# Column-quarter matmuls of a decoder step's sample group, issued in fours

## The chip, the cores and the metric

The kernel runs on one core of a Trainium2 chip. The metric is the device time of one execution in microseconds (us), from the core's first instruction to its last and what lies around them; lower is better. TensorE (PE) multiplies and transposes, VectorE (DVE), ScalarE (ACT) and GpSimd (POOL) work on elements, SyncE (SP) issues most of the DMAs.

## The reference

One step of a decoder layer for two groups that share the weights: a prompt group (1 x 1024 tokens, positions 0 to 1023) and a sample group (8 samples x 4 tokens, each with a past of 512 positions in pages of 128, and 256 memory tokens of its own). All inputs are float32.

```python
def layer_forward(x, p, layer, h0_re, h0_im, conv_prev, mem_k, mem_v, attend):
    xn = rms_norm(x, p['ln1_g'])
    proj = xn @ p['w_in']
    ...
    ssm_out, h_re, h_im = s5_mixer(u, h0_re, h0_im, p)
    ...
    o = attend(q, k, v, lam)
    o = rms_norm(o, p['subln_g']) * (1.0 - lam0)
    mixed = jnp.concatenate([ssm_out, o.reshape(bsz, t, ATTN_WIDTH)], axis=-1)
    x = x + mixed @ p['w_out']
    xn = rms_norm(x, p['ln2_g'])
    cq = rms_norm((xn @ p['ca_wq']).reshape(bsz, t, CA_HEADS, CA_HEAD_DIM), p['ca_q_norm_g'])
    s = jnp.einsum('bqhd,bmhd->bhqm', cq, mem_k.astype(cq.dtype)).astype(f32) * (CA_HEAD_DIM ** -0.5)
    pr = jax.nn.softmax(s, axis=-1).astype(x.dtype)
    co = jnp.einsum('bhqm,bmhd->bqhd', pr, mem_v.astype(x.dtype)).reshape(bsz, t, D_MODEL)
    x = x + co @ p['ca_wo']
    ...
    x = x + (jax.nn.silu(conv) * (xn @ p['ffn_wv'])) @ p['ffn_wd']
    return x, k, v, h_re, h_im, buf[:, t:]
```

`attend` is differential attention with 4 heads of two maps: softmax of each map, the first less `lam` times the second, times the values. For the sample group, keys and values are the 4 pages that the page table names, and the 4 new tokens.

## The kernel before, in words

The program is written as generators ("streams"). Each yields a cost after a piece of work, and a driver takes next a piece of the stream that is furthest behind its rate; a scheduler then puts the instructions of each engine in an order of their own, and each engine works through its order strictly. A stream's place in the driver decides roughly where its instructions come to lie, its tiles' buffers decide when its loads can start.

The prompt group's large matmuls run as three passes of a shortened float32 format, 128 x 128 weights over 256 to 512 columns (`mm3`, lines 180 to 182). The sample group's attention is done in full float32, and its stationary operand has 32 columns for each sample (4 heads x 2 maps x 4 tokens, or 4 heads x 4 tokens padded): the matmul of sample b uses one quarter of TensorE's columns, `tile_position=(0, 32 * (b % 4))`, and writes 32 partitions of the result. A float32 matmul is recorded as two passes. Four places do this:

- `keys` (line 1369), in `sample_attention`: for each of two groups `s` of four samples and for each sample, two pages at a time. A page is gathered by SP (`pg`, five buffers `PGB`), TensorE transposes it into `pt`, ScalarE copies that to `KT`, and after every second page four matmuls (one a head) of 256 columns accumulate the scores `Sp`.
- `values` (line 1422), for each sample, four pages (also `pg`) and the new tokens `vs_`: five matmuls of 512 columns accumulate `Op`, each issued as its page comes. `values(0)` runs beside `keys(1)`; `soft` lies between keys and values of a group.
- `sample_keys` (line 1784), cross-attention, for each of four heads and each sample: the memory keys `kt` (three buffers) are loaded by SP, transposed, copied to `KT` by ScalarE; two matmuls of 256 columns accumulate `Ssm`.
- `sample_values` (line 1857), cross-attention's output: 32 loads of `vt`, 128 x 512 each, issued by GpSimd, six ahead; each has one matmul of 512 columns into `Op` (line 1870).

Beside the first two run the prompt's last attention heads, the memory's keys and values (`memory_kv`, `pjm`, whose weights `mraw` come by SP) and the state-space scan (`yp`, `wp`, `kp`); beside the third the prompt's cross-attention (`pp`, `S`, `po`); beside the fourth the output projection (`wo_stage`, `pp`), whose last third waits for `sample_values`. The matmuls of `kp` (line 965, `ssm_setup`) use column quarters too: they go through the four quarters with two matmuls on each.

Of the kernel before, what the change touches and what calls it, by code (L numbers as in the profile page):

```python
# [21 lines left out]
NS = 32  # L22
# [16 lines left out]
TB = [(0, 384), (384, 384), (768, 288)]  # L39
TILES = [(128 * t, 128) for t in range(8)] + [(1024, 32)]  # L40


class Boosted:
    """An engine whose instructions the scheduler ranks boost[0] places earlier."""
# [23 lines left out]
def hymba_step(ctx: ExitStack, tc: tile.TileContext, A: dict, O: dict, upto=99, dbg=None):  # L68
# [7 lines left out]
    def par(*streams):  # L76
        # each stream: a generator of costs, its rate, the share it starts behind, its boost
# [109 lines left out]
    class Carve:  # L187
        """Small tiles cut from a few large ones; a tag names one region."""
# [132 lines left out]
    def ssm_params(st, ps):  # L321
# [58 lines left out]
        # cos and sin of the chunk angle times 0..15, and times 0, 16, ..., 112  # L380
# [725 lines left out]
    # sample group: the recurrence step by step  # L1106
# [77 lines left out]
    # keys and values of the prompt's memory  # L1184
# [78 lines left out]
    # differential attention of the sample group over its pages  # L1263
    sc = {}

    def sample_tables(sa):
# [29 lines left out]
        # columns: the past, new keys for the first four samples, new keys for the last four  # L1296
# [46 lines left out]
    def sample_attention(sa):  # L1343
# [6 lines left out]
        def gather(src, j):  # L1350
            g = sa.tile([128, 512], F32, tag="pg", name="pg", bufs=PGB)
# [17 lines left out]
        def keys(s):  # L1369
            Sp = ps_j.tile([128, PAST], F32, tag="pjb", name="Sp")  # L1370
            Sps.append(Sp)
            for b4 in range(4):
                b = 4 * s + b4
                rows = slice(32 * b4, 32 * b4 + 32)
                for pg in range(NPG):
                    if pg % 2 == 0:
                        KT = sa.tile([128, NH, 256], F32, tag="KT", name="KT", bufs=2)
                    kp_ = gather(kpg, NPG * b + pg)
# [3 lines left out]
                    c = 128 * (pg % 2)  # L1382
                    nc.scalar.copy(KT[:, :, c:c + 128], pt.rearrange("p (h k) -> p h k", h=4))
                    yield 440
                    if pg % 2:
# [219 lines left out]
    if upto <= 4:  # L1605
        return

# [1 line left out]
    pcs = ctx.enter_context(ExitStack())  # L1609
    cqs = pool(pcs, "cqs", 1)  # L1610
    hm = cqs.tile([128, 4], F32, name="hm")
# [499 lines left out]
```

## Time and profile before

| | before |
|---|---|
| device time, median of 3 runs | 1912.89 us (1910.13 to 1913.94) |
| span of the profiled execution, which the page gives as its time | 1912.4 us |
| TensorE busy (weight loads) | 1842.9 us (1649.2 us) |
| VectorE, ScalarE, GpSimd busy | 1144.4, 623.8, 473.8 us |
| moved by DMA | 147.15 MB, mean 77 GB/s |
| mean granted TensorE clock | 0.966 of full speed |

A pass counts as busy until its modelled end, and passes overlap, so a busy share says that TensorE had work and not how much it could have done. The runs of before lie within 0.2% of each other.

### The profile page before, as it was taken

The numbers are of one execution on the slowest core, as the hardware profiler recorded it, in microseconds if no ns is written. First come the engines' busy times: TensorE is split into PE (matmuls) and PEld (weight loads), VectorE is DVE, ScalarE is ACT, GpSimd is POOL, SyncE is SP. The second block draws the span as 40 slices with busy tenths as digits, with TensorE's granted clock in tenths as the row PEclk, the third lists the DMA queues.
The fourth block names the chain that finished last, engine by engine and source line by source line (L and its number), as shares of the span: only waits on it lengthen the run. The fifth ranks groups of instructions, "written<-read, shape, count | busy, mean of one in ns | idle before, by whom it ended". The sixth has DMA issues, their size and how long they took to land. (4 is left out here: it accounts for less than half of the span.)

```text
span 1912.4 us, 29088 instructions
## 1 busy us (share of the span) xinstructions
PE 1842.9 (96%) x11105; PEld 1649.2 (86%) x11105; DVE 1144.4 (60%) x2867; ACT 623.8 (33%) x1425; POOL 473.8 (25%) x547
## 2 busy tenths in 40 slices
PE   7899999889899999999989999999999999999998
PEld 6787897767556799888855999999999999999998
DVE  6976448795876554655452665555656646556554
ACT  6654345545243543344441312112102102112112
POOL 4412321360530024100012333223123123223200
PEclk8888998979799999999999999999999999999999
DMA  7202112134355342322243111011111102102102
GB/s 224 68 28 62 44 48 65 48 108 129 113 147 158 117 145 82 95 85 92 78 154 127 56 37 56 27 52 57 45 34 57 55 23 68 45 23 68 45 23 92
DMA packets 160773, 147.15 MB, mean 77 GB/s; under 512 B 14167, under 2 KB 142067, under 8 KB 160634
## 3 DMA queue, kind: packets, MB, share of 16 engines
q1 hardware_dynamic: 135698, 111.03, 19.2%
q0 software_dynamic: 7232, 18.71, 3.2%
q10 hardware_dynamic: 17704, 15.56, 2.4%
q8 instruction: 87, 1.43, 0.3%
q14 instruction: 52, 0.43, 0.1%
HBM read 120.07 MB, written 25.19 MB: 76 GB/s over the span
## 5 line engine op out<-in xcount | busy, mean ns | idle before, releaser
L54 DVE TENSOR_TENSOR xacc<-xacc,pd 128x384 f32<-128x384 f32 (+1 forms) x264 | 134.9, 518 | 168.7 <-PE pd L182 168.7
L54 ACT CAST whi<-raw 128x1024 fp32r<-128x1024 f32 x74 | 77.5, 1049 | 427.9 <-PE pg L181 332.8
L182 PE MATMUL pv<-Xh,wlo 128*128 128x384 f32 (+1 forms) x528 | 171.3, 325 | 0.3 <-DVE wlo L54 0.3
L180 PE MATMUL pv<-Xh,whi 128*128 128x384 f32 (+1 forms) x528 | 171.6, 325 | 0.0
L180 PE MATMUL pd<-ah,dhi 128*128 128x384 f32 (+1 forms) x528 | 171.2, 325 | 0.1
L180 PE MATMUL pg<-Xh,whi 128*128 128x384 f32 (+1 forms) x528 | 171.2, 324 | 0.0
L181 PE MATMUL pv<-Xl,whi 128*128 128x384 f32 (+1 forms) x528 | 171.1, 324 | 0.0
L182 PE MATMUL pd<-ah,dlo 128*128 128x384 f32 (+1 forms) x528 | 170.9, 324 | 0.0
L181 PE MATMUL pd<-al,dhi 128*128 128x384 f32 (+1 forms) x528 | 170.1, 322 | 0.5 <-DVE al L54 0.5
L181 PE MATMUL pg<-Xl,whi 128*128 128x384 f32 (+1 forms) x528 | 170.6, 323 | 0.0
L182 PE MATMUL pg<-Xh,wlo 128*128 128x384 f32 (+1 forms) x528 | 170.2, 322 | 0.0
L54 DVE TENSOR_TENSOR wlo<-raw,whi 128x1024 fp32r<-128x1024 f32 x74 | 107.0, 1448 | 21.1 <-ACT whi L54 20.8
L180 PE MATMUL pp<-Mh,whi 128*128 128x384 f32 (+1 forms) x336 | 109.2, 328 | 0.9 <-ACT Mh L54 0.9
L181 PE MATMUL pp<-Ml,whi 128*128 128x384 f32 (+1 forms) x336 | 108.5, 326 | 0.8 <-DVE Ml L54 0.8
L182 PE MATMUL pp<-Mh,wlo 128*128 128x384 f32 (+1 forms) x336 | 109.2, 327 | 0.0
L798 POOL TENSOR_TENSOR raw<-raw,GT 128x1024 f32<-128x1024 f32 x30 | 67.0, 2233 | 165.2 <-DMA raw<-in_ffn_wg_dram 99.2
L180 PE MATMUL pj<-whi,Xh 128*128 128x384 f32 (+1 forms) x288 | 105.3, 367 | 1.5 <-DVE mx L54 1.5
L181 PE MATMUL pj<-wlo,Xh 128*128 128x384 f32 (+1 forms) x288 | 103.2, 359 | 0.2
L182 PE MATMUL pj<-whi,Xl 128*128 128x384 f32 (+1 forms) x288 | 103.2, 359 | 0.0
L182 PEld LDWEIGHTS pv<-Xh,wlo 128*128 128x128 f32 x528 | 99.7, 189 | 0.5 <-DVE wlo L54 0.4
L181 PEld LDWEIGHTS pd<-al,dhi 128*128 128x128 f32 x528 | 99.2, 188 | 0.8 <-DVE al L54 0.8
L180 PEld LDWEIGHTS pd<-ah,dhi 128*128 128x128 f32 x528 | 99.0, 188 | 0.9 <-ACT ah L54 0.5
(813 smaller groups left out, 4873.8 us busy)
## 6 DMA issues: line engine op xcount, KB each, us to landing
raw<-in_ffn_wg_dram SPq DMA_DIRECT2D x22, 512.0 KB, 3.8
raw<-in_ffn_wv_dram SPq DMA_DIRECT2D x22, 512.0 KB, 3.8
raw<-in_ffn_wd_dram SPq DMA_DIRECT2D x22, 512.0 KB, 3.6
pg<-in_cache_k_dram SPq DMA_DIRECT2D x32, 256.0 KB, 2.7
pg<-in_cache_v_dram SPq DMA_DIRECT2D x32, 256.0 KB, 3.3
kt<-in_cache_mem_k_dram SPq DMA_DIRECT2D x32, 256.0 KB, 2.8
vt<-in_cache_mem_v_dram POOLq DMA_DIRECT2D x32, 256.0 KB, 3.9
raw<-in_w_in_dram SPq DMA_DIRECT2D x48, 128.0 KB, 2.5
```

The lines of the kernel that those rows point to most:

```text
L54: return f(*a, **k)
L180: nc.tensor.matmul(out, lhsT=wh, rhs=xh, start=start, stop=False)
L181: nc.tensor.matmul(out, lhsT=wh, rhs=xl, start=False, stop=False)
L182: nc.tensor.matmul(out, lhsT=wl, rhs=xh, start=False, stop=stop)
L798: nc.gpsimd.tensor_tensor(out=raw, in0=raw, in1=g.unsqueeze(2).to_broadcast([128, KD, 128]), op=ALU.mult)
```

## The change

Each of the four places now collects the operands of four samples and then issues their matmuls in fours, one on each column quarter, in the order 3, 2, 1, 0 (`QUADS`), under a raised scheduling priority.

- `keys`: the loop over pages is outside, that over the four samples inside. `KT` holds one page of four samples (8 KB a partition); 16 matmuls of 128 columns follow each quad of pages. `pg` has two buffers and not five; `KT`, `V` and `Pm` share one tag, `big`, with two buffers (`KTB`).
- `values`: `V` holds one page of four samples, gathered by four loads; then four matmuls of 512 columns, one a sample.
- `sample_keys`: `KT` holds the keys of four samples in one buffer (`CKB`, which the tile names), `kt` has two buffers and not three, then eight matmuls of 256 columns. `co` has two buffers and not three.
- `sample_values`: 16 loads of 512 KB with four samples x 256 columns (runs of 1 KB in memory and not 2 KB), three buffers, then four matmuls of 256 columns.

The number of transposes, copies and bytes is the same. The diff, cut to these (what is left out are comments):

```diff
@@ -37,11 +37,12 @@
+QUADS = (3, 2, 1, 0)
@@ -1347,8 +1348,9 @@
         npg = A['cache_k'].shape[1]
         pages = {}
 
-        def gather(src, j):
-            g = sa.tile([128, 512], F32, tag="pg", name="pg", bufs=PGB)
+        def gather(src, j, g=None):
+            if g is None:
+                g = sa.tile([128, 512], F32, tag="pg", name="pg", bufs=PGB)
             if j not in pages:
                 pages[j] = nc.sync.value_load(ptab[0:1, j:j + 1], min_val=0, max_val=npg - 1)
             nc.sync.dma_start(out=g, in_=src[bass.ds(pages[j], 1)].rearrange("n s f -> (n s) f"))
@@ -1369,29 +1371,26 @@
         def keys(s):
             Sp = ps_j.tile([128, PAST], F32, tag="pjb", name="Sp")
             Sps.append(Sp)
-            for b4 in range(4):
-                b = 4 * s + b4
-                rows = slice(32 * b4, 32 * b4 + 32)
-                for pg in range(NPG):
-                    if pg % 2 == 0:
-                        KT = sa.tile([128, NH, 256], F32, tag="KT", name="KT", bufs=2)
-                    kp_ = gather(kpg, NPG * b + pg)
+            for pg in range(NPG):
+                KT = sa.tile([128, 4, NH, 128], F32, tag="big", name="KT", bufs=KTB)
+                for b4 in range(4):
+                    kp_ = gather(kpg, NPG * (4 * s + b4) + pg)
                     pt = tp("pt", "td")
                     for h in range(NH):
                         nc.tensor.transpose(pt[:, 128 * h:128 * h + 128], kp_[:, 128 * h:128 * h + 128], ident)
-                    c = 128 * (pg % 2)
-                    nc.scalar.copy(KT[:, :, c:c + 128], pt.rearrange("p (h k) -> p h k", h=4))
+                    nc.scalar.copy(KT[:, b4], pt.rearrange("p (h k) -> p h k", h=4))
                     yield 440
-                    if pg % 2:
-                        for h in range(NH):
-                            nc.tensor.matmul(Sp[rows, 256 * (pg // 2):256 * (pg // 2) + 256], lhsT=Qb[:, h, b, :],
-                                             rhs=KT[:, h, :], start=h == 0, stop=h == NH - 1,
-                                             tile_position=(0, 32 * b4))
-                        yield 500
+                with tc.high_priority():
+                    for h in range(NH):
+                        for b4 in QUADS:
+                            nc.tensor.matmul(Sp[32 * b4:32 * b4 + 32, 128 * pg:128 * pg + 128],
+                                             lhsT=Qb[:, h, 4 * s + b4, :], rhs=KT[:, b4, h, :],
+                                             start=h == 0, stop=h == NH - 1, tile_position=(0, 32 * b4))
+                yield 1000
 
         def soft(s):
             Sp = Sps[s]
-            Pm = sa.tile([128, PAST + NS], F32, tag="Pm", name="Pm")
+            Pm = sa.tile([128, PAST + NS], F32, tag="big", name="Pm", bufs=KTB)
             mx = sa.tile([128, 1], F32, tag="mxs", name="mxs")
             sm_ = sa.tile([128, 1], F32, tag="sms", name="sms")
             mx2 = sa.tile([128, 2], F32, tag="mx2", name="mx2")
@@ -1423,16 +1422,19 @@
             aT = aTs[s]
             yield from until(lambda: 'left' in done)
             Op = ps_x.tile([128, 512], F32, tag="x", name="Op")
-            for b4 in range(4):
-                b = 4 * s + b4
-                for pg in range(NPG + 1):
-                    if pg < NPG:
-                        lh, rh = aT[:, pg, 32 * b4:32 * b4 + 32], gather(vpg, NPG * b + pg)
-                    else:
-                        lh, rh = aT[:NS, NPG, 32 * b4:32 * b4 + 32], vs_
-                    nc.tensor.matmul(Op[32 * b4:32 * b4 + 32, :], lhsT=lh, rhs=rh, start=pg == 0, stop=pg == NPG,
-                                     tile_position=(0, 32 * b4))
-                    yield 240
+            for pg in range(NPG + 1):
+                if pg < NPG:
+                    V = sa.tile([128, 4, 512], F32, tag="big", name="V", bufs=KTB)
+                    rh = [gather(vpg, NPG * (4 * s + b4) + pg, V[:, b4]) for b4 in range(4)]
+                else:
+                    rh = [vs_] * 4
+                yield 10
+                with tc.high_priority():
+                    for b4 in QUADS:
+                        lh = aT[:128 if pg < NPG else NS, pg, 32 * b4:32 * b4 + 32]
+                        nc.tensor.matmul(Op[32 * b4:32 * b4 + 32, :], lhsT=lh, rhs=rh[b4], start=pg == 0,
+                                         stop=pg == NPG, tile_position=(0, 32 * b4))
+                yield 950
             os_ = gp.tile([128, 128], F32, tag="os_", name="os_")
             nc.vector.tensor_scalar(out=os_, in0=Op[:, 0:128], scalar1=hmask[:, 0:1], scalar2=None, op0=ALU.mult)
             for h in range(1, NH):
@@ -1473,7 +1475,7 @@
-    PGB = 5
+    PGB, KTB = 2, 2
@@ -1625,6 +1627,7 @@
+        CKB = 1
@@ -1775,7 +1778,7 @@
                         split(co_h[z][:, t0:t0 + nq], co_l[z][:, t0:t0 + nq], po[:, :nq])
                         yield 6 * nq / 2.4
                         continue
-                    co = ca.tile([128, 384], F32, tag="co", name="co", bufs=3)
+                    co = ca.tile([128, 384], F32, tag="co", name="co", bufs=2)
                     nc.scalar.copy(co[:, :nq], po[:, :nq])
                     d = 256 * h + 128 * z
                     nc.scalar.dma_start(out=coT[d:d + 128, t0:t0 + nq], in_=co[:, :nq])
@@ -1784,22 +1787,25 @@
         def sample_keys(h):
             while h not in queries:
                 yield None
-            for b in range(NB):
-                kt = ca.tile([128, 2, 256], F32, tag="kt", name="kt", bufs=3)
-                nc.sync.dma_start(out=kt, in_=A['cache_mem_k'][0, b, :, h, :].rearrange("(c p) d -> p c d", p=128))
-                pt = ps_t.tile([128, 2, 2, 128], F32, tag="tp", name="pt")
-                for c in range(2):
+            for s in range(2):
+                KT = ca.tile([128, 4, 2, NMEM], F32, tag="KT", name="KT", bufs=CKB)
+                for b4 in range(4):
+                    kt = ca.tile([128, 2, 256], F32, tag="kt", name="kt", bufs=2)
+                    nc.sync.dma_start(out=kt, in_=A['cache_mem_k'][0, 4 * s + b4, :, h, :].rearrange(
+                        "(c p) d -> p c d", p=128))
+                    pt = ps_t.tile([128, 2, 2, 128], F32, tag="tp", name="pt")
+                    for c in range(2):
+                        for z in range(2):
+                            nc.tensor.transpose(pt[:, z, c, :], kt[:, c, 128 * z:128 * z + 128], ident)
+                    nc.scalar.copy(KT[:, b4].rearrange("p z m -> p (z m)"), pt.rearrange("p z c m -> p (z c m)"))
+                    yield 440
+                with tc.high_priority():
                     for z in range(2):
-                        nc.tensor.transpose(pt[:, z, c, :], kt[:, c, 128 * z:128 * z + 128], ident)
-                KT = ca.tile([128, 2, NMEM], F32, tag="KT", name="KT")
-                nc.scalar.copy(KT.rearrange("p z m -> p (z m)"), pt.rearrange("p z c m -> p (z c m)"))
-                yield 440
-                r = 32 * (b % 4)
-                for z in range(2):
-                    nc.tensor.matmul(Ssm[r:r + 32, :], lhsT=Qc[:, z, b, :], rhs=KT[:, z, :],
-                                     start=h == 0 and b < 4 and z == 0, stop=h == NH - 1 and b >= 4 and z == 1,
-                                     tile_position=(0, r))
-                yield 240
+                        for b4 in QUADS:
+                            nc.tensor.matmul(Ssm[32 * b4:32 * b4 + 32, :], lhsT=Qc[:, z, 4 * s + b4, :],
+                                             rhs=KT[:, b4, z, :], start=h == 0 and s == 0 and z == 0,
+                                             stop=h == NH - 1 and s == 1 and z == 1, tile_position=(0, 32 * b4))
+                yield 960
 
         def field_masks():
             pio = ca.tile([128, 1], I32, name="pio", bufs=1)
@@ -1856,24 +1862,26 @@
 
         def sample_values():
             Op = ps_o.tile([128, 1024], F32, name="Op")
-            work = [(s, c, g, b4) for s in range(2) for c in range(2) for g in range(2) for b4 in range(4)]
-
-            def load(s, c, g, b4):
-                vt = wx.tile([128, 512], F32, tag="vt", name="vt", bufs=7)
-                nc.gpsimd.dma_start(out=vt, in_=A['cache_mem_v'][0, 4 * s + b4, 128 * c:128 * c + 128].rearrange(
-                    "m h d -> m (h d)")[:, 512 * g:512 * g + 512])
+            work = [(g, s, c) for g in range(NH) for s in range(2) for c in range(2)]
+
+            def load(g, s, c):
+                vt = wx.tile([128, 4, 256], F32, tag="vt", name="vt", bufs=3)
+                nc.gpsimd.dma_start(out=vt, in_=A['cache_mem_v'][0, 4 * s:4 * s + 4, 128 * c:128 * c + 128].rearrange(
+                    "b m h d -> m b (h d)")[:, :, 256 * g:256 * g + 256])
                 return vt
 
-            vts = [load(*w) for w in work[:6]]
+            vts = [load(*w) for w in work[:3]]
             yield WD
-            for i, (s, c, g, b4) in enumerate(work):
-                nc.tensor.matmul(Op[32 * b4:32 * b4 + 32, 512 * g:512 * g + 512],
-                                 lhsT=PT[:, c, s, 32 * b4:32 * b4 + 32], rhs=vts[i],
-                                 start=s == 0 and c == 0, stop=s == 1 and c == 1, tile_position=(0, 32 * b4))
-                if i + 6 < len(work):
-                    vts.append(load(*work[i + 6]))
-                yield 250
-            os_ = wx.tile([128, 256], F32, tag="vt", name="os_", bufs=7)
+            for i, (g, s, c) in enumerate(work):
+                with tc.high_priority():
+                    for b4 in QUADS:
+                        nc.tensor.matmul(Op[32 * b4:32 * b4 + 32, 256 * g:256 * g + 256],
+                                         lhsT=PT[:, c, s, 32 * b4:32 * b4 + 32], rhs=vts[i][:, b4],
+                                         start=s == 0 and c == 0, stop=s == 1 and c == 1, tile_position=(0, 32 * b4))
+                if i + 3 < len(work):
+                    vts.append(load(*work[i + 3]))
+                yield 500
+            os_ = wx.tile([128, 256], F32, tag="os", name="os_", bufs=1)
             nc.vector.tensor_scalar(out=os_, in0=Op[:, 0:256], scalar1=hm[:, 0:1], scalar2=None, op0=ALU.mult)
             for h in range(1, NH):
                 nc.vector.scalar_tensor_tensor(out=os_, in0=Op[:, 256 * h:256 * h + 256], scalar=hm[:, h:h + 1],
```

How it moves instructions on TensorE is seen in its order, at two places. The first is in the second half of the attention values (`values(1)`); line 1433 is the matmul `Op` of before, `pjm` is `memory_kv`, `tp` and `fp` are of the scan. Before:

```order
L1433 MATMUL Op<-pg,aT 32x512
L182 MATMUL pjm<-mwh,ml 128x256
L180 MATMUL pjm<-mwh,mh 128x256
L181 MATMUL pjm<-mwl,mh 128x256
L1433 MATMUL Op<-pg,aT 32x512
L1433 MATMUL Op<-vs__78,aT 32x512
L182 MATMUL pjm<-mwh,ml 128x256
L1096 MATMUL fp<-ident,fin 16x128
L1073 MATMUL tp__7272<-ident,yt 128x128 x2
L1433 MATMUL Op<-pg,aT 32x512
```

With the change the matmul has line 1435, `yp` is of the scan:

```order
L1054 MATMUL yp<-CLi,Hi 128x128
L1435 MATMUL Op<-V,aT 32x512 x4
L1074 MATMUL tp__7304<-ident,yt 128x128 x4
L1074 MATMUL tp__7313<-ident,yt 128x128 x4
L1435 MATMUL Op<-V,aT 32x512 x4
L1435 MATMUL Op<-vs__78,aT 32x512 x4
```

The matmuls of four samples now stand in one row, where single ones stood between others; the two `V` rows are the quads of the third and the fourth page, and the quad of the second page stands ten rows further up.

The second place is the cross-attention's output; `pp` is the output projection. Before:

```order
L181 MATMUL pp<-Ml_11060,whi 128x384
L182 MATMUL pp<-Mh_11054,wlo 128x384
L1870 MATMUL Op<-vt,PT 32x512 x2
L180 MATMUL pp<-coh_8580,whi 128x384
L181 MATMUL pp<-col_8582,whi 128x384
L182 MATMUL pp<-coh_8580,wlo 128x384
L180 MATMUL pp<-coh_8581,whi 128x384
L180 MATMUL pp<-Mh_11055,whi 128x384
L181 MATMUL pp<-col_8583,whi 128x384
L1870 MATMUL Op<-vt,PT 32x512
L182 MATMUL pp<-coh_8581,wlo 128x384
```

With the change, where the first quads stand:

```order
L1878 MATMUL Op<-vt,PT 32x256 x4
L181 MATMUL pp<-Mh_11061,whi 128x384
L182 MATMUL pp<-Ml_11067,whi 128x384
L183 MATMUL pp<-Mh_11061,wlo 128x384
L181 MATMUL pp<-Mh_11062,whi 128x384
L182 MATMUL pp<-Ml_11068,whi 128x384
L183 MATMUL pp<-Mh_11062,wlo 128x384
L1878 MATMUL Op<-vt,PT 32x256 x4
L181 MATMUL pp<-Mh_11063,whi 128x384
L182 MATMUL pp<-Ml_11069,whi 128x384
L183 MATMUL pp<-Mh_11063,wlo 128x384
L1878 MATMUL Op<-vt,PT 32x256 x4
```

Every quad needs one `vt` of 512 KB; the next three stand 28 rows further on, so that three buffers are refilled while some 36 `pp` matmuls run.

## Rows read from the trace of the kernel before

**Rows 1.** The page's busy time, share of the span and instructions of each engine.

```profile
PE 1842.9 (96%) x11105; PEld 1649.2 (86%) x11105; DVE 1144.4 (60%) x2867; ACT 623.8 (33%) x1425; POOL 473.8 (25%) x547
```

**Rows 2.** By line: passes, ns min/median/max, first and last start us, form.

```profile
L1387 PE MATMUL Sp<-KT,Qb x128: 378/379/637, 401.0 to 566.3; 128*32 128x256 f32 x128
L1433 PE MATMUL Op<-pg,aT x64: 592/592/617, 547.0 to 639.9; 128*32 128x512 f32 x64
L1433 PE MATMUL Op<-vs__78,aT x16: 587/600/612, 557.1 to 640.9; 32*32 32x512 f32 x16
L1799 PE MATMUL Ssm<-KT,Qc x128: 379/379/403, 806.9 to 981.8; 128*32 128x256 f32 x128
```

**Rows 3.** TensorE's timeline: start us, us, engine, line, operation, tiles, columns, count.

```profile
1032.09 0.33 PE L182 MATMUL pp<-coh,wlo 128*128 128x384 f32 x1
1032.35 1.05 PE L1870 MATMUL Op<-vt,PT 128*32 128x512 f32 x2
1033.33 0.44 PE L180 MATMUL pp<-Mh,whi 128*128 128x384 f32 x1
1033.61 0.33 PE L181 MATMUL pp<-Ml,whi 128*128 128x384 f32 x1
1033.78 0.34 PE L182 MATMUL pp<-Mh,wlo 128*128 128x384 f32 x1
```

**Rows 4.** The same timeline, around 1014 us.

```profile
1014.26 1.06 PE L1870 MATMUL Op<-vt,PT 128*32 128x512 f32 x6
1015.25 0.44 PE L182 MATMUL pp<-Mh,wlo 128*128 128x384 f32 x1
```

**Rows 5.** The same timeline, around 452 us.

```profile
451.53 0.45 PE L965 MATMUL kp<-CLr,Bbr 128*32 128x128 f32 x8
451.77 0.42 PE L965 MATMUL kp<-CLi,Bbi 128*32 128x128 f32 x8
452.02 1.89 PE L1387 MATMUL Sp<-KT,Qb 128*32 128x256 f32 x8
```

**Rows 6.** By stretch: length; PE, PEld, DVE, ACT, POOL busy; clock; DMA share; GB/s.

```profile
400.00:440.00 40.00, 36.31 (x211) 26.59 (x210) 36.70 (x86) 20.90 (x49) 26.39 (x23) 0.87 0.42 135
440.00:480.00 40.00, 39.19 (x313) 32.93 (x313) 19.47 (x67) 20.06 (x41) 2.44 (x3) 1.00 0.38 115
480.00:510.00 30.00, 20.63 (x116) 13.62 (x114) 28.96 (x62) 7.13 (x16) 14.27 (x14) 0.78 0.41 128
510.00:650.00 140.00, 139.86 (x837) 88.76 (x838) 89.64 (x200) 55.94 (x101) 29.34 (x24) 0.95 0.47 144
800.00:950.00 150.00, 148.75 (x947) 128.44 (x947) 75.74 (x297) 63.24 (x153) 4.40 (x5) 1.00 0.27 87
950.00:988.00 38.00, 31.50 (x187) 23.84 (x185) 22.30 (x94) 18.46 (x46) 3.84 (x7) 0.96 0.30 90
988.00:1054.00 66.00, 65.83 (x238) 33.83 (x239) 18.81 (x37) 13.49 (x30) 18.46 (x30) 0.97 0.47 159
```

**Rows 7.** By stretch, line 1387 alone (two rows), then line 1799 alone.

```profile
440.00:480.00 40.00, 7.63 (x32) 3.27 (x32) 1.00 0.38 115
510.00:650.00 140.00, 13.16 (x48) 5.31 (x48) 0.95 0.47 144
...
800.00:950.00 150.00, 25.22 (x96) 8.58 (x96) 1.00 0.27 87
```

**Rows 8.** DMA issues: transfer, queue, count, KB each, median us from issue to landing.

```profile
pg<-in_cache_k_dram SPq DMA_DIRECT2D x32, 256.0 KB, 2.7
pg<-in_cache_v_dram SPq DMA_DIRECT2D x32, 256.0 KB, 3.3
vt<-in_cache_mem_v_dram POOLq DMA_DIRECT2D x32, 256.0 KB, 3.9
raw<-in_ca_wo_dram SPq DMA_DIRECT2D x8, 512.0 KB, 4.1
```

**Rows 9.** GpSimd's issues of `vt`: ns min/median/max, first and last start us.

```profile
L1863 POOL DMA_DIRECT2D vt<-in_cache_mem_v_dram x32: 537/537/642, 983.5 to 1038.7; - x32
```

## The prediction

> **What bounds the kernel now.** I read the page's totals first: TensorE is busy for 96% of the span [rows 1]. A total hides the stages, so the next view was the four groups of matmuls that the change touches [rows 2]. Each float32 matmul of the program stands there as two passes: 128 passes of 256 columns for `Sp`, 64 + 16 of 512 for the attention values, 128 of 256 for `Ssm`; the 32 matmuls of 512 for the cross-attention values make 64 more ([rows 3] show one such pair). The third view was the table by stretch [rows 6]. From 440 to 480 us, 510 to 650, 800 to 950 and 988 to 1054, TensorE is busy for 39.2 of 40, 139.9 of 140, 148.8 of 150 and 65.8 of 66 us: there it is the bound, since VectorE is busy for half to two thirds of the time or less. From 400 to 440 and 480 to 510 VectorE is the bound (36.7 of 40, 29.0 of 30), and TensorE waits; from 950 to 988 neither is full.
>
> **What one pass costs.** Eight passes of `Sp` take 1.89 us and one alone 0.38 [rows 5, 2], so passes on one column quarter follow each other after (1.89 - 0.38) / 7 = 0.216 us, whatever the 96 idle columns do. A pass of 512 columns costs twice that, 0.43. Going in and out costs too: in [rows 3] two passes stand between full-width matmuls that follow each other after 0.17 us. From 1032.09 to 1033.61 are 1.52 us; less two such matmuls (0.34) and two passes (0.86), 0.32 us are left for one interruption.
>
> **Do quarters run side by side?** This is the central step, and the trace already answers it. At 1014.26 the order put three `Op` matmuls of three different samples side by side by chance: six passes, and the next matmul starts 0.99 us later [rows 4], where one such matmul alone holds TensorE for 0.98 (1032.35 to 1033.33, [rows 3]). For four quarters, `kp` issues eight matmuls of 128 columns, two per quarter: 16 passes in 0.49 us, from 451.53 to 452.02 [rows 5]. In line they would be 16 x 0.108 = 1.73 us; four quarters at once give 4 x 0.108 = 0.43. So I take a fourth of the streaming time. The bounds are the whole time (no overlap) and a fourth.
>
> A page speaks against it, for matmuls of two passes. The Trainium skill, "TensorE: Matmul & The Clock Gate", Part 3, The mechanism, says that matmuls start and end strictly in program order and that a weight load goes ahead of running matmuls only where the row group differs; these quarters share their rows. By that rule the second pass of one sample would hold back the next sample, and a round of eight passes would take four to five pass times and not two. The six passes in 0.99 us and the 16 in 0.49 contradict it.
>
> **The sum at full overlap.** Streaming before: 128 x 0.216 = 27.6 us (`Sp`), 80 x 0.43 = 34.4 (attention values), 27.6 (`Ssm`), 64 x 0.43 = 27.5 (cross values): 117.1. The order has them in 16, 23, 30 and 29 runs, 98 interruptions of 0.32 = 31.4. After: 29.3 of streaming (the same columns, in halves for `Sp` and the cross values, over four quarters), and 8, 8, 8 and 16 runs, 40 x 0.32 = 12.8. So `Sp` goes from 32.7 to 9.5 us (-23.2), the attention values from 41.8 to 11.2 (-30.6), `Ssm` from 37.2 to 9.5 (-27.7), the cross values from 36.8 to 12.0 (-24.8): 106.3 us of TensorE's time. Transposes, copies and bytes stay as they are.
>
> **What of it shortens the span**, stretch by stretch. Of the 128 passes of `Sp`, 32 lie in 440 to 480 and 48 in 510 to 650; of those of `Ssm`, 96 in 800 to 950 [rows 7]. The other 48 of `Sp` lie in the two stretches in which VectorE is full.
> - 400 to 440 and 480 to 510 (8.7 us): VectorE is full, so nothing: 0.
> - 440 to 480: 5.8, TensorE full; I take 5.
> - 510 to 650: 8.7 + 30.6 = 39.3. Here the change adds a wait. A `V` buffer now holds four pages, and its four loads start only when the quad before has left it. One page lands in 3.3 us, 512 KB in 4.1 [rows 8]: 0.8 more per 256 KB, so 1 MB in about 5.7 us (an estimate from these two). In the order only thirteen rows, some 5 us of work, stand between the last quad of the second half and the quad that frees its buffer, so it is a little late; others have 30 rows or more. Bounds: 0, and 8 quads x 5.7 = 46 us. I take 1 us a quad: 39 becomes 32. The gathers queue on SP, so the loads of `mraw` behind them wait as well.
> - Keys: `pg` has two buffers where it had five, with a landing of 2.7 us [rows 8]; bounds 0, and every second page waited for in full, 16 x 2.7 = 43. The order leaves mostly 20 to 40 rows between a page's transposes and those of the next but one, which is more than 2.7 us, so 0.
> - 800 to 950: 27.7 x 96 / 128 = 20.8. `kt` goes from three buffers to two (256 KB as a key page, so bounds 0 and 43 again), `KT` to one, refilled by ScalarE, which is idle for over half of the stretch. I take 19.
> - 950 to 988: 6.9 possible; TensorE waits there for the softmax of the last head. I take 2.
> - 988 to 1054: 24.8 possible. 159 GB/s over 66 us are 10.5 MB; in 41 us that is 256 GB/s, far more than in any of these stretches. Issuing a `vt` costs GpSimd 0.54 us [rows 9]; with four row pieces per partition it costs between 0.54 and 2.15. A load needs then up to 2.15 + 3.9 + 0.8 = 6.9 us [rows 8, 9], and its buffer comes round every three quads, 36 matmuls x 0.17 + 3 x 0.75 = 8.4 us: it fits, with little to spare. Bounds: no wait, and the whole gain lost. The first quad also needs 512 KB before it starts where 256 KB did. I take 15.
>
> The sum is 5 + 32 + 19 + 2 + 15 = 73 us. The span of the profiled execution is 1912.4; the median of the runs is 1912.9, half a us above it, so I carry nothing over: 1912.9 - 73 = **1840 us**.
>
> **Rivals.**
> - *Operand waits take half of it back.* The waits above come near the middle of their bounds: 510 to 650 keeps 15 of 39, 988 to 1054 keeps 3. With 5 + 19 + 2 the gain is 44, the time 1869; at worst 15 to 45, 1868 to 1898. For it: SP's and GpSimd's queues are in order and the buffers fewer. Against it: traffic uses 47% of the DMA engines' time.
> - *Passes keep program order* (the page's rule). Streaming is halved only: 58.5 + 18.6 of interruptions = 77 of 106 us; with the same yield (73 of 106) that is 53, 1860. Against it: [rows 4, 5].
> - *The quads bring no overlap, or TensorE's time is not the bound.* Only interruptions are saved, 18.6 x 0.69 = 13: 1900. That the rows of TensorE are full speaks against it.
> - *Slower:* two key buffers. TensorE is in order, and a transpose whose page is late holds all else. If every second page, every second `kt` and every `V` quad is waited for in full, 43 + 43 + 46 = 132 us come on top, more than the 106 saved: about +26, 1939. It decides where the work between a transpose and the next but one falls under 2.7 us; in one place (three pages transposed in a row with two buffers) it does, but TensorE is waiting for VectorE there anyway.
>
> **Chances.** The forecast (gain 50 to 90, so 1823 to 1863) 0.66; nearly all converted (1806 to 1823) 0.07; operand waits 0.14; program order 0.05; no overlap 0.03; slower 0.05. The forecast with part of its neighbours gives the range, 1818 to 1874. A change within 0.2% (4 us, about what a measurement of this kernel can tell from none) needs savings and waits to cancel, 0.02 out of the operand waits; faster 0.93, slower 0.05.
>
> **What the profile would show.** Right: `Sp` x32 passes in about 1 us, `Ssm` x16 in about 1, an `Op` quad x8 of 512 columns in about 1, of 256 in about 0.6; TensorE's total lower by about 75 to 100 us; the stretch of the last `Op` about 50 us long and no longer 66. Wrong: quads that last 1.7 us or more (program order); TensorE idle ahead of `pt<-ident,pg`, `Op<-V` or `Op<-vt`, released by a DMA, for more than some 20 us in sum; or a granted clock that falls below 0.9 in these stretches, as it does from 480 to 510 where TensorE waits (0.78).

## The result and the profile after

The changed kernel takes 1866.0 us (median of 4 runs, 1861.29 to 1870.42) where the kernel before, on the same chip, takes 1912.45: 46.5 us less, a ratio of 0.9762 [0.9742, 0.9782]. The forecast was 1840. The profiled execution of after has a span of 1866.8 us, 45.6 less than that of before.

The page's busy time answers to [rows 1]: TensorE lost 78.6 us, inside the 75 to 100 that were named.

```profile
PE 1764.3 (95%) x11297; PEld 1640.4 (88%) x11297; DVE 1154.4 (62%) x2867; ACT 623.8 (33%) x1425; POOL 470.0 (25%) x531
```

TensorE's timeline of after (start us, us until the modelled end, engine, line, operation, tiles, columns, count) shows one quad of each of the four places and what follows it, against [rows 3 to 5].

```profile
455.58 1.08 PE L1386 MATMUL Sp<-KT,Qb 128*32 128x128 f32 x32
456.50 0.44 PE L966 MATMUL kp<-CLr,Bbr 128*32 128x128 f32 x8
...
603.59 1.07 PE L1435 MATMUL Op<-V,aT 128*32 128x512 f32 x8
604.49 0.38 PE L1416 MATMUL pn<-Sw,Pm 128*32 128x128 f32 x2
...
948.04 1.07 PE L1805 MATMUL Ssm<-KT,Qc 128*32 128x256 f32 x16 [0.46 <-ACT KT L55]
949.04 0.44 PE L181 MATMUL po<-Ph,cvh 128*128 128x384 f32 x1
...
1004.00 0.64 PE L1878 MATMUL Op<-vt,PT 128*32 128x256 f32 x8
1004.57 0.44 PE L181 MATMUL pp<-Mh,whi 128*128 128x384 f32 x1
```

From start to next start these are 0.92, 0.90, 1.00 and 0.57 us: four quarters run at once, as forecast. Added up in the same way over all runs of such matmuls, the four places held TensorE for 32.5, 37.1, 30.8 and 29.0 us before and hold it for 10.6, 10.6, 8.0 and 10.1 now, 90 us less. The forecast had 106 by another measure: its price of 0.32 us for an interruption holds 0.2 that the neighbours lose (0.26 and 0.28 us where 0.17 is usual, [rows 3]), and a run counted from its start to the next start leaves that out. So about half of what TensorE was spared reached the span. The table by stretch (length; PE, PEld, DVE, ACT, POOL busy; granted clock; DMA share; GB/s) answers to [rows 6]; the ends of the stretches have moved with the program.

```profile
400.00:440.00 40.00, 29.84 (x185) 23.05 (x185) 33.34 (x78) 19.48 (x45) 26.97 (x22) 0.73 0.35 114
440.00:480.00 40.00, 37.16 (x363) 33.20 (x362) 19.49 (x69) 19.88 (x39) 2.45 (x3) 0.88 0.41 122
480.00:510.00 30.00, 16.48 (x134) 13.25 (x132) 26.25 (x52) 7.19 (x15) 13.18 (x12) 0.79 0.35 113
510.00:627.00 117.00, 107.08 (x893) 83.79 (x894) 99.40 (x206) 54.06 (x98) 27.75 (x25) 0.92 0.59 183
783.00:930.00 147.00, 140.25 (x987) 131.32 (x985) 82.44 (x328) 69.69 (x166) 3.47 (x4) 0.98 0.32 99
930.00:959.00 29.00, 19.80 (x131) 14.72 (x134) 14.77 (x56) 12.14 (x33) 2.29 (x3) 0.92 0.32 96
959.00:1005.00 46.00, 46.00 (x307) 34.03 (x300) 20.26 (x37) 12.99 (x29) 15.09 (x18) 0.94 0.66 215
```

Rows of TensorE that were full before have gaps now (37.2 of 40, 107.1 of 117), and from 440 to 480 us the clock is 0.88 and no longer 1.00. Only the last stretch is still full, 46 us long where it had 66.

For a balance I cut the program at four events that both kernels have: the first `pn<-ksT` (the group's attention begins), the first `zp` of the projection behind it, the first transpose of `kt`, and the first `Op<-vt`; the last stage ends where the feed-forward part begins (`pg<-Xh`). The same table has these rows for the attention and the cross-attention scores, before:

```profile
389.30:646.10 256.80, 240.08 (x1553) 165.29 (x1553) 182.28 (x430) 104.93 (x208) 76.15 (x66) 0.92 0.44 135
...
803.00:988.20 185.20, 177.28 (x1111) 149.34 (x1110) 95.04 (x381) 80.54 (x197) 7.32 (x11) 0.99 0.28 90
```

and after:

```profile
386.30:626.70 240.40, 201.38 (x1681) 162.36 (x1681) 191.51 (x431) 106.13 (x210) 74.15 (x66) 0.85 0.48 148
...
783.30:958.60 175.30, 159.35 (x1114) 145.56 (x1112) 96.92 (x382) 81.53 (x198) 5.76 (x7) 0.97 0.32 98
```

| stage | before | after | gained | forecast |
|---|---|---|---|---|
| attention | 256.8 | 240.4 | 16.4 | 5 + 32 |
| projection (untouched) | 156.9 | 156.6 | 0.3 | 0 |
| cross-attention scores | 185.2 | 175.3 | 9.9 | 19 + 2 |
| cross-attention values | 130.3 | 112.5 | 17.8 | 15 |

The other 1.2 us lie ahead of these stages and behind them. In the attention stage the runs of `Sp` and `Op` shrank by 48.4 us. TensorE's idle time rose from 16.7 to 39.0 us, and the time in which it worked at half clock (the clock's records laid over those of the matmuls) from 35.3 to 58.6; half clock costs half of its length. So -48.4 + 22.3 + 11.7 = -14.4, near the measured -16.4. For the scores the same sum is -22.8 + 8.0 + 3.3 = -11.5, measured -9.9. The gain was made, and then idle time and the clock took back two thirds of it in the attention and half of it in the scores. Who makes TensorE wait in the attention stage is in the table of waits (us in total, times, longest), after:

```profile
PE yp L1051 <- DVE Hr L55: 9.2, 1, 9.2
PE S L181 <- DVE mx L55: 5.9, 2, 4.9
PE pt L725 <- DVE aTl L55: 4.3, 1, 4.3
PE sp L979 <- ACT Kt L55: 4.1, 2, 2.2
PE pt L1380 <- DMA pg<-in_cache_k_dram: 3.2, 1, 3.2
...
PE Op L1435 <- DMA V<-in_cache_v_dram: 2.2, 2, 1.7
```

All waits of this view add up to the 39.0 us of idle time; before, they add up to 16.8, and the first two were:

```profile
PE S L180 <- DVE mx L54: 5.3, 3, 2.6
PE yp L1050 <- DVE Hr L54: 4.4, 1, 4.4
```

Loads of the sample group's operands stand for 5.4 us only; the longest single wait is for the state-space scan on VectorE (`Hr`), and it is 4.8 us longer than before, while that for the softmax's maxima (`mx`) is nearly as before. The chain of waits tells it otherwise, though. From 559 to 581 us it reads (start us, us, what):

```profile
559.46 1.12 PE Op L1435 x8
...
562.16 5.47 DMA V<-in_cache_v_dram
567.65 4.80 DMA V<-in_cache_v_dram
572.47 5.32 DMA V<-in_cache_v_dram
577.84 2.80 PE Op L1435 x16
```

A quad frees its `V` buffer, and then the last loads of three quads follow each other for 15.6 us. Counted from its first issue, such a quad's four loads took 7.0 to 8.8 us here; the prediction's estimate was 5.7. Thus two views named two suspects, and the experiments had to say which of them held the gain back.

### The profile page after: what moved, and what is told of

It reads as the page before. It is cut to its first block, busy times and chain, and to the rows that moved or that the text cites. A ratio compares the mean times of both kernels' runs of the same rounds, so it can differ in the third digit from the quotient of the medians.

```text
span 1866.8 us, 29420 instructions
## 1 busy us (share of the span) xinstructions
PE 1764.3 (95%) x11297; PEld 1640.4 (88%) x11297; DVE 1154.4 (62%) x2867; ACT 623.8 (33%) x1425; POOL 470.0 (25%) x531
## 4 chain that ended last, share of the span: by engine, by line
PE 81%; DVE 10%; DMA 2%; ACT 2%; issue 1%; SPq 0%; POOL 0%; DVEq 0%; ACTq 0%; POOLq 0%
PE pp L181 5%; PE pp L182 5%; PE pp L183 5%; PE pv L183 5%; PE pv L181 5%; PE pv L182 5%; PE pd L183 5%; PE pd L182 4%; PE pd L181 4%; PE pg L181 4%; PE pg L182 4%; PE pg L183 4%; PE pj L181 2%; PE pj L183 2%; PE pj L182 2%; PE S L181 2%
```

## The experiments

All ratios are to the kernel before, in runs on the same chip.

**One half of the change at a time.** The first kernel has the quads in keys and values only, the second in the cross-attention only.

```diff
 e1: cross-attention as before
-            for s in range(2):
-                KT = ca.tile([128, 4, 2, NMEM], F32, tag="KT", name="KT", bufs=CKB)
+            for b in range(NB):
+                kt = ca.tile([128, 2, 256], F32, tag="kt", name="kt", bufs=3)
...
 e2: keys and values as before, PGB = 5
-            for pg in range(NPG):
-                KT = sa.tile([128, 4, NH, 128], F32, tag="big", name="KT", bufs=KTB)
+            for b4 in range(4):
...
```

> Quads in keys and values alone; both cross-attention parts as before. Theory (the stage to 627 us gave only 19 of the 37 us that were forecast for it, since VectorE is nearly full there): the gain is about 19 us, 1893 us, and the attention stage ends near 627 us. Rival (the stage gives what was forecast and the cross-attention parts lose): a gain of 35 us or more, 1877 us or less.

> Quads in the two cross-attention parts alone; keys and values as before. Theory: the gains add up, so 46 less 19 is 27 us here, 1885 us: 10 from the stage with Ssm, 18 from the one with vt. Rival (the parts disturb each other through the order): the two gains together differ from 46 us by more than 8.

They take 1895.2 us, a ratio of 0.9918 [0.9887, 0.9949], and 1878.6, 0.9825 [0.98, 0.9851]: 17 and 34 us less, together 51 against 46 for both, which is the sum within the intervals. The attention stage of the first is 240.7 us long, the later stages of the second 174.9 and 108.5. So the two halves don't hinder each other, and the attention's half is the one that yields little: 17 of its 48.

**The same arrangement without the overlap.** Each matmul gets all four samples' columns (128), so that no two can run at once. The values differ: every sample's rows get the sum over the four samples.

```diff
-                            nc.tensor.matmul(Sp[32 * b4:32 * b4 + 32, 128 * pg:128 * pg + 128],
-                                             lhsT=Qb[:, h, 4 * s + b4, :], rhs=KT[:, b4, h, :],
-                                             start=h == 0, stop=h == NH - 1, tile_position=(0, 32 * b4))
+                            nc.tensor.matmul(Sp[:, 128 * pg:128 * pg + 128], lhsT=fl(Qb[:, h, 4 * s:4 * s + 4, :]),
+                                             rhs=KT[:, b4, h, :], start=h == 0 and b4 == 3,
+                                             stop=h == NH - 1 and b4 == 0)
...
```

> The changed kernel with its loads, buffers and rows, but each of the four matmuls of a quad uses all 128 columns, so that they cannot lie side by side (the four samples' queries meet each sample's keys, so values differ). Streaming goes from 29 back to 117 us, the interruptions stay few. Theory (the side-by-side passes are what was gained, with a part lost in waits that stays lost): 50 to 75 us longer than the changed kernel, 1916 to 1940. Rival (the gain came from the fewer interruptions, or from the new order of work): within 10 us of the changed kernel, 1866 to 1876.

1923.68 us, 1.0068 [1.0042, 1.0093]: 58 more than with the overlap. The row of its attention stage:

```profile
386.50:662.90 276.40, 250.46 (x1681) 201.14 (x1681) 191.17 (x432) 108.35 (x214) 75.23 (x66) 0.86 0.43 133
```

Here `Sp` and `Op` hold TensorE for 32.9 and 35.1 us, nearly as before the change, yet the stage is 19.6 us longer than before. So collecting four samples, with its fewer buffers and its other order, costs about 20 us in the attention (which of them costs it isn't told apart); the overlap then brings 36 back. In the scores and the values the overlap is worth 12 and 11 us.

**Quads sample by sample.** The same matmuls in the same quad, but all of one sample's before the next one's.

```diff
-                    for h in range(NH):
-                        for b4 in QUADS:
+                    for b4 in QUADS:
+                        for h in range(NH):
...
```

> The changed kernel, but the 16 matmuls of a key quad and the 8 of a memory-key quad go sample by sample (all heads of one sample, then the next) and not in fours. Theory from kp's 16 passes in 0.49 us: TensorE looks far enough ahead, runs of one quarter overlap with the next ones, a key quad still takes about 1 us and the time is the changed kernel's, within 3 us. Rival (only neighbours in the order overlap, or passes keep program order): a key quad takes 2 us or more, and the time is 10 to 30 us longer.

1873.38 us, 0.98 [0.9765, 0.9835]: by the ratios 7 us longer than the changed kernel, with intervals that overlap. The key quad decides more clearly. The timeline has one of this kernel:

```profile
472.83 2.46 PE L1386 MATMUL Sp<-KT,Qb 128*32 128x128 f32 x32
475.22 0.39 PE L181 MATMUL pjm<-mwh,mh 128*128 128x256 f32 x1
```

It lasts 2.39 us: more than the 0.92 of the order in fours, less than the 3.5 of 32 passes after one another (32 x 0.108). So the theory's "about 1 us" fails for the key quad, and the rival's "2 us or more" came without its 10 to 30 us. How far a quarter runs ahead is seen in the table by stretch for the `Sp` line alone (PE's passes in brackets), in a quad at half clock that starts at 411.05 and has eight passes per quarter:

```profile
411.04:411.90 0.86, 0.85 (x4) 0.71 (x5) 0.50 0.00 0
411.90:412.76 0.86, 0.86 (x9) 0.73 (x8) 0.50 0.11 29
```

In the first 0.86 us four passes start, one after another. In the next 0.86 it is eight, two at a time (a ninth still runs from before): the next quarter's first pass starts with the fifth of the eight, past three that still wait. (The trace doesn't name a pass's quarter; this takes the order to be the one written.) `Ssm`, with four passes per quarter, keeps its full overlap: 1.02 us a quad and 1.00 with the order in fours, at full clock. Four of its passes start within 0.04 us, so the fourth quarter starts past nine waiting passes, three in each of the other quarters; `kp` has done the same [rows 5]. What is short, then, is the row of passes of one quarter that may wait. The rule that was set against the forecast, that matmuls start strictly in program order (the Trainium skill, "TensorE: Matmul & The Clock Gate", Part 3, The mechanism), doesn't hold here: by it, the second quarter could not start before the eighth pass. Nor does an engine work "through its order strictly", as the part ahead of the prediction says, where TensorE's passes lie on different quarters. The order in fours is worth some 1.5 us of TensorE's time a key quad.

**Fewer loads.** If the `V` loads on the chain, or the two page buffers, hold the gain back, leaving three of four loads out must return it. All four samples then share one sample's pages, of the values in the first kernel, of the keys in the second.

```diff
 e5
-                    rh = [gather(vpg, NPG * (4 * s + b4) + pg, V[:, b4]) for b4 in range(4)]
+                    rh = [gather(vpg, NPG * 4 * s + pg, V[:, 0])] * 4
 e10
+                kp_ = gather(kpg, NPG * 4 * s + pg)
                 for b4 in range(4):
-                    kp_ = gather(kpg, NPG * (4 * s + b4) + pg)
```

> The changed kernel with one value page of four loaded for each quad and used for all four samples (24 of the 32 value loads left out, values differ). The run with full-width matmuls showed the attention stage 20 us longer than before for the same streaming, so the new arrangement costs about 20 us there. Theory A (V quads wait for their four loads, two buffers): 8 to 15 us shorter than the changed kernel, 1851 to 1858. Theory B (VectorE's work and the order decide): within 4 us of it, 1862 to 1870.

> The changed kernel with one key page of four loaded for each quad and transposed four times (24 of the 32 key loads left out, values differ). Theory A (two page buffers where there were five: transposes wait, TensorE's clock falls): 5 to 15 us shorter than the changed kernel, 1851 to 1861. Theory B: within 4 us of it, 1862 to 1870.

1867.98 us, 0.9761 [0.9735, 0.9787], and 1872.22, 0.979 [0.9752, 0.9828]: neither is faster than the changed kernel. The attention stage of the first kernel:

```profile
388.40:628.70 240.30, 204.68 (x1681) 164.06 (x1681) 191.35 (x430) 106.57 (x213) 74.57 (x66) 0.84 0.41 126
```

It is 240.3 us long, to 0.1 us as long as with all loads. In the chain from 540 to 630 us the `V` loads fell from 23.4% to 3.2%, and matmuls took their place. A load that lies on the chain is not by itself the bound if another chain of almost the same length runs beside it. Value and key loads were not left out together.

**Less for VectorE.** The second suspect is VectorE, whose chain `Hr` belongs to. Of the attention stage it works for 191.5 of 240.4 us. The low halves of 16 weight blocks of `memory_kv` are not computed, the high halves stand in for them; in the changed kernel and in that of before.

```diff
-                    lo = wr.tile([128, 4, 256], F32R, tag="wloa", name="mwl")
-                    split(hi, lo, raw)
-                    ws.append((hi, lo))
+                    nc.scalar.copy(hi, raw)
+                    ws.append((hi, hi))
```

> The changed kernel without the 16 low parts of memory_kv's weights (the high part is used twice, values differ): 16 VectorE instructions of 1.22 us, 20 us, are gone, 11 of them in the stretch in which VectorE is over 90% busy. Theory B (VectorE bounds the attention stage of the changed kernel): 8 to 18 us shorter, 1848 to 1858. Theory A (loads): within 4 us, 1862 to 1870.

> The kernel before without the same 16 VectorE instructions. Theory B: TensorE bounds that stage before, so the cut brings less here than in the changed kernel, 0 to 6 us, 1906 to 1912. Rival (VectorE's chain bounds the stage before as well): as much as there, 8 us or more.

1864.84 us, 0.9757 [0.9739, 0.9776], and 1916.66, 1.0026 [1.0008, 1.0044]. In the first VectorE has 30 us less to do in the attention stage, and the whole is the same; the stage is 237.5 us long, 2.9 less. The second is 5 us longer than the kernel before, which neither of its forecasts had. The table by stretch of that kernel has a part that shows where the rest may have gone:

```profile
530.00:540.00 10.00, 9.91 (x74) 7.54 (x72) 10.00 (x28) 4.95 (x11) 1.47 (x3) 1.00 0.68 213
540.00:550.00 10.00, 7.03 (x93) 4.96 (x96) 9.96 (x15) 3.23 (x6) 8.87 (x7) 1.00 0.70 212
550.00:560.00 10.00, 6.47 (x33) 2.84 (x25) 9.00 (x30) 3.58 (x5) 0.56 (x1) 0.66 0.74 191
560.00:570.00 10.00, 10.00 (x42) 5.21 (x43) 6.02 (x19) 1.89 (x4) 0.20 (x1) 0.56 0.27 92
570.00:580.00 10.00, 10.00 (x39) 8.43 (x39) 6.24 (x18) 2.14 (x5) 0.00 (x0) 0.50 0.20 68
```

From 540 to 560 us VectorE is full or nearly so (10.0 and 9.0 of 10) and TensorE idle for a third of the time; within that the clock falls to half (1.2 of 2.4 GHz) and stays there for most of the next 20, in which TensorE is the one that is full. Two pairs of passes of `yp` on the chain of the same kernel have the price:

```profile
571.54 0.72 PE yp L1051 x2
...
617.85 0.41 PE yp L1051 x2
```

At half clock such a pair takes 0.72 us, at full clock 0.41. Over the stage TensorE's idle time fell by 9.0 us to 30.0, but half clock under work is 69.6 us where the changed kernel has 58.6.

**Less for TensorE.** Is TensorE's time the bound of this stage at all? Of the three passes of `memory_kv` only the first is left, 256 passes of 256 columns less; at the 0.12 us from one to the next that is 31 us of TensorE. In the kernel of before, some 27 of these 31 us lie from 440 to 480 and 510 to 650 us, where its row was full.

```diff
-                        mm3(pj[:, t], mh[b][:, kk, sl], ml[b][:, kk, sl], hi[:, kk], lo[:, kk], k == 0, k == KD - 1)
+                        nc.tensor.matmul(pj[:, t], lhsT=mh[b][:, kk, sl], rhs=hi[:, kk], start=k == 0, stop=k == KD - 1)
```

> The changed kernel with one of three passes of memory_kv's matmuls (two of three left out on TensorE, some 57 us at 0.12 us each at most 31 us of them streaming; VectorE's splits stay; the memory's keys and values lose accuracy). Theory C (in the changed kernel the attention stage is held by waits between engines and by the clock that falls with them; its TensorE work is no longer the bound): 0 to 10 us shorter than the changed kernel, 1856 to 1866. Rival (TensorE's work is still the bound): 20 to 31 us shorter, 1835 to 1846.

> The kernel before with the same passes left out. Theory C: there TensorE was the bound, so more comes off than in the changed kernel: 15 to 30 us shorter than before, 1882 to 1897. Rival: as little as in the changed kernel, within 10 us of before.

In the changed kernel 1857.12 us, 0.9727 [0.9691, 0.9763]: by the ratios 7 less than with all passes, with intervals that just overlap. Its attention stage is 225.1 us long, 15.3 less for 31 us of work (the projection behind it takes 2.2 more), and it runs at a clock of 0.75, for 93.3 us at half clock under work:

```profile
389.20:614.30 225.10, 185.72 (x1393) 141.76 (x1393) 189.57 (x429) 107.07 (x212) 73.23 (x66) 0.75 0.49 149
```

In the kernel of before 1907.39, 0.9988 [0.9974, 1.0003]: 3 us, which can't be told from none. Its attention stage:

```profile
386.00:636.20 250.20, 219.62 (x1297) 140.75 (x1297) 189.17 (x446) 106.78 (x212) 77.74 (x66) 0.88 0.47 143
```

31 us of TensorE's work are gone, the stage is 6.6 us shorter; the idle time rose from 16.7 to 30.6 us, the time at half clock under work from 35.3 to 50.1, and the clock fell from 0.92 to 0.88. This is the central finding: already before the change TensorE's work alone did not set this stage's length, although its row was full from 510 to 650 us. The theory that I held until then, that TensorE was the bound before and ceased to be it, falls. One reserve: both kernels keep `yield 320`, by which the driver paces this stream, for a third of the work; an order made for the shorter stream was not tried.

**Without the priority.** The four blocks lose their raised priority.

```diff
-                with tc.high_priority():
+                if True:
```

> The changed kernel without the raised priority of the quads. Theory C: the priority is not what makes TensorE wait; within 6 us of the changed kernel, 1860 to 1872, TensorE idle for 33 to 45 us of the attention stage. Rival (quads that are put forward stand in TensorE's order ahead of work that could run): 8 us or more shorter, TensorE's idle time in that stage under 30 us.

1866.65 us, 0.98 [0.9761, 0.984]: the same within the intervals, and TensorE is idle for 39.7 us of the attention stage, as Theory C said.

**Quads in the keys alone.** Values and cross-attention are as before, the page buffers stay at two.

```diff
-                    V = sa.tile([128, 4, 512], F32, tag="big", name="V", bufs=KTB)
-                    rh = [gather(vpg, NPG * (4 * s + b4) + pg, V[:, b4]) for b4 in range(4)]
...
+                        lh, rh = aT[:, pg, 32 * b4:32 * b4 + 32], gather(vpg, NPG * b + pg)
```

> Quads in keys alone; values sample by sample as before, but from two page buffers where it had five; cross-attention as before. Theory C (the key quads free TensorE mostly where it waits anyway): 0 to 8 us shorter than before, 1904 to 1912, the rest of the stage's 17 us being the values'. Rival (the keys bring their 22 us and the values' quads lose): 12 us or more shorter, 1900 or less.

1943.22 us, 1.0184 [1.0163, 1.0204]: 33 more than the kernel before, which neither theory had. The table of waits from 540 to 700 us, for SP's queue:

```profile
SPq L1356 <- PE Op L1432: 76.7, 26, 15.8
```

By line, its issues of the value pages, with the first and the last start:

```profile
L1356 SPq DMA_DIRECT2D pg<-in_cache_v_dram x32: 332/333/739, 549.3 to 686.9; - x32
```

In the kernel before, the same two views have:

```profile
SPq L1354 <- PE Op L1433: 34.8, 24, 7.5
```

```profile
L1354 SPq DMA_DIRECT2D pg<-in_cache_v_dram x32: 332/333/565, 539.6 to 626.8; - x32
```

With two buffers SP waits 77 us for `Op` to leave a page, and the 32 loads are spread over 138 us instead of 87. Over the attention and the projection behind it, which take 33.3 us more, TensorE's idle time rises from 19.6 to 54.5 us. That fits a loss by two page buffers as large as the slower rival's (1939), with the values though, and not with the keys as it said; in the changed kernel `V` takes four pages at once. It was read and not tested: the new order of the keys and the buffers were not changed apart. Which of the later transfers in SP's queue does the damage isn't settled.

## Why the prediction was right, and where it was not

**The passes.** Right: against the full-width matmuls of the third experiment a quad is about a fourth as long at three places and 0.57 us against 1.54 at the fourth (8 passes of 256 columns, where going in and out weighs more); the overlap was there as the chance neighbours and `kp` [rows 4, 5] had shown, and without it the kernel is 58 us slower. Program order, as a rival, falls with the quads of about 1 us and with the experiment sample by sample. The words "TensorE is in order" are too wide where passes lie on different quarters; that a transpose whose page is late holds all else was not tested.

**The operand waits.** Forecast small and small: 8.3 us in all (`pg` 3.2, `V` 2.2, `kt` 1.5, `vt` 1.4). Leaving out three quarters of the value or key loads returned nothing, so neither alone took the gain, and this rival isn't borne out, though the time lies close to its 1868 to 1898: a time near a rival's doesn't show its cause. The landings of a page became longer against [rows 8]:

```profile
pg<-in_cache_k_dram SPq DMA_DIRECT2D x32, 256.0 KB, 3.3
V<-in_cache_v_dram SPq DMA_DIRECT2D x32, 256.0 KB, 4.5
...
vt<-in_cache_mem_v_dram POOLq DMA_DIRECT2D x16, 512.0 KB, 5.4
```

**The cross-attention values.** 15 forecast, 17.8 measured. The issue of a `vt` in four pieces costs GpSimd 0.75 us against 0.54 [rows 9], near the lower bound:

```profile
L1869 POOL DMA_DIRECT2D vt<-in_cache_mem_v_dram x16: 751/751/797, 953.0 to 999.7; - x16
```

**The yield, the step that failed.** The gain of 46.5 us lies below the 50 to 90 that the forecast gave itself; the range of 1818 to 1874 holds the time because it takes in a part of the rivals, and that is luck as far as the mechanism goes. The prediction said of 440 to 480, 510 to 650 and 800 to 950 us that TensorE is full, "there it is the bound", and carried TensorE's saving over to the span almost whole: 37 us for the attention, of which 16.4 came, and 21 for the scores, of which 9.9 came. These two fell 32 us short; the values gave 3 more than forecast and 1.5 came elsewhere, which makes the 27 us between 73 and 45.6. For the attention the runs show what stands in its place. A full row didn't mean that TensorE's work set the time: 31 us of it taken out of the kernel before shortened the stage by 6.6 and the whole by 3. That the work had merely been spread over the time that other chains needed is my reading of it. Of the 48.4 us that the quads freed, 22.3 became waiting, mostly on VectorE's and ScalarE's steps (`Hr` and `Kt` of the scan, `aTl` of the prompt's attention) and for 5.4 us on loads, and some 11.7 went to the clock, which spent 23.3 us more at half under work. The prediction had named the sign (a clock below 0.9 where TensorE was full), and from 440 to 480 us it is 0.88; it gave it no price. It also put no cost on the new arrangement besides the waits for loads; that cost is about 20 us in the attention. The forecast of 73 was thus too high by the yield of two stages, and its 1840 missed by 26 us.

For the scores the shortfall was read, not tested. TensorE's idle time rose by 8.0 us, of which 5.5 lie where its row had been full (6.8 idle of 147 us, where it had 1.3 of 147), in many waits of 0.5 us for ScalarE's and VectorE's results; in the last 29 us, where the last head's steps follow each other, it is idle for 9.2, where before it was for 6.7 of 38. Half clock under work, none before in that first part, is 6.8 us there now. One kernel with the quads in the cross-attention alone has the same length (174.9 us).

**What stays open.** Which chain sets the attention's 240 us. The loads, VectorE's splits and the priority were each taken away alone, and the stage stayed between 237 and 248 us; no two of them were taken away together, and more buffers were not tried. Every edit also makes the scheduler order the whole program anew, so a few us between such kernels say little. None of the kernels that compute all of it is faster than the changed one.

## What to carry to other kernels

A full row of TensorE doesn't prove that its work is the bound where many chains meet: thin out some neighbouring TensorE work first, and see whether the stage gets shorter. Count the gain of a faster part by stage, and price the idle time and the lower clock that may follow it. Matmuls on different column quarters run at once if they are issued in turn (here also with up to four passes of one quarter in a row); what is paid for it in buffers and order can be half of the gain, as here 20 of 36 us in the attention.

## What the hardware showed that was not expected

The next quarter's matmuls start past three waiting passes of a quarter, not past more of the same one: eight passes per quarter in sample order gave 2.39 us a quad, four per quarter kept the whole overlap. And a faster stage can run at a lower clock: with `Sp` and `Op` in less than a third of their time, the mean clock of the attention stage fell from 0.92 to 0.85, the time at half clock under work from 35.3 to 58.6 us.
